# A hybrid decoder step on one core: token halves of 512 and 520 in the seven-product scheme, other PSUM chains, no sums on GpSimd from the gated part on

## The chip, the cores and the metric

The kernel runs on one core of one Trainium2 chip, in one launch. The metric is the device time in microseconds. A program of this kernel keeps five engines in step by semaphores: TensorE (PE; the weight loads are listed apart as PEld), VectorE (DVE), ScalarE (ACT), GpSimd (POOL) and SyncE (SP, which here only issues DMAs).

## What is computed

One decoder layer for a prompt of 1024 tokens and 8 sample tokens (1032 columns in all), with D_MODEL = 1024 and a feed-forward width D_FF = 2816, in float32:

```python
h = rmsnorm(x, g_mix); u = h @ w_in                       # pool branch, conv branch (value, gate)
ya = pool_mixer(...); yb = conv_mixer(...)                # windows of 2/4/8/16; width-31 depthwise conv, LayerNorm, swish
x = x + concatenate([ya, yb]) @ w_out
x = x + cross_attn(rmsnorm(x, g_attn), mk, mv, w_q, w_o)  # 4 heads, 256 memory tokens
h = rmsnorm(x, g_ffn)
x = x + (silu(h @ w_gate) * (h @ w_up)) @ w_down
y = rmsnorm(x, g_final)                                   # also returned: new pool/conv states, memory keys and values
```

## The kernel before

Channels lie on the 128 partitions, tokens on the free axis: first the 512 even prompt tokens, then the 512 odd ones, then the 8 samples. A matrix product takes a weight block of 128x128 as the stationary operand and a stretch of tokens as the moving one. Each float32 operand is split into a high part and a low rest, and each product is three passes (`PASSES`: high x high, high x low, low x high), so each block of a product is three MATMULs per stretch of tokens. `split` (L363 for the high part, L374 for the rest) makes the two parts on ACT, DVE or GpSimd; `split_by_dma` (L385, L392) makes the rest by two ACT passes and a DMA that GpSimd issues and that adds the original in memory.

The program has four stages.

- **Early.** Input projection, pooling, convolution, output projection, attention with its own small path for the samples, and the projection `w_o` (`proj_o`, tile `po`). Most products here take 1032 tokens as three stretches of 344 (tiles `ps`, `oa`, `ob`, `po`, line L471). Keys and values of the memory are products of 256 and 512 columns (tiles `kps`, L841, and `vps`, L918).
- **Gated** (`first_two`, `sixth`, `others` for the first two feed-forward tiles, `seven` for the other twenty). Gate and up projection of one feed-forward tile of 128 channels are a 2x2 block product: two halves of the 1024 input channels, two halves of the 1032 tokens, outputs gate and up. The scheme of Strassen and Winograd makes it of seven products in place of eight, each of 4 weight blocks, three passes and 516 tokens. A product's 516 tokens are two MATMULs of 258 (`TQ`) into two PSUM banks. The products are named A11, A12, A22, S1 to S4, after their token blocks (tiles `ab`, by index: 0 A12, 1 A22, 2 S4, 3 S1, 4 A11, 5 S2, 6 S3). Sums of weights (`wTa`, `wTb`) and of products make up for the missing eighth.
- **Down** (`down`, 16 units: 4 chunks of hidden channels, `c`, by 4 pairs of output tiles, `p`). The first 2048 hidden channels go through the same scheme with w_down: seven products of two weight blocks each, tiles `pr` from `hb` (hidden blocks read back from DRAM) with `dW` (plain weights) and `dV` (summed weights). The results gather in `x2` (printed `x` or `x_0` to `x_3`) and `pp`.
- **Last** (`last_down`, `final`). The other six hidden tiles (`ho`) go through plain products (tile `fd`) in three spans of tokens, `LAST_SPANS`, each followed by its final norm and stores.

The order on every engine is made at build time. The program first lists tasks, each with the engines that could run it and a cost; `Program.order` then walks a model of time, and gives each engine its next task by readiness, room in the buffers and priority. `ORDER` lists the pieces of the early stage; `BIAS`, `LEAD`, `SLACK` and `MARGINS` set how early weights are fetched and prepared and how far costs are trusted. A task that may run on DVE or GpSimd goes where the model ends it first. PSUM has eight banks: two buffers `mm` of three banks and two `ms` of one bank. `product` takes an `mm` buffer, or each third time two `ms` buffers ("narrow", one per 258 tokens); with `onto` it adds a second product onto a PSUM buffer that still holds an earlier one, after the earlier sum has been read out.

Lines that matter below: L1312 is the MATMUL of `product`, L1646 that of `last_down`; L1328 is the DVE instruction that reads a product from PSUM and adds it to a sum, L1332 the ACT copy from PSUM; L1336 (`combine`) and L1354 (`times`) are sums and products of two SBUF operands; L1266 the sums of gate and up weights, L1487 those of the down weights.

## Time and profile before

| | us |
|---|---|
| median of 3 runs (1241.48 to 1244.19) | 1242.89 |
| time of the profiled execution | 1243.26 |
| its span, first to last instruction | 1241.5 |
| PE busy in the span | 1213.6 |
| DVE busy | 887.5 |
| ACT busy | 540.2 |
| GpSimd busy | 461.5 |

The profiled execution's time is 1.8 us above its span. The page gives busy time by engine, the span in 40 slices, the DMA queues, the chain that ended last and groups of instructions; the trace answers further questions by window, by line, by tile and by wait. A busy PE is one with MATMULs in flight, back to back or not: how fast they follow each other must be read from a count of instructions in a stretch.

### The profile page before, as it was taken

The numbers are of one execution on the slowest core, as the hardware profiler recorded it, in microseconds if no ns is written. First come the engines' busy times: TensorE is split into PE (matmuls) and PEld (weight loads), VectorE is DVE, ScalarE is ACT, GpSimd is POOL, SyncE is SP. The second block draws the span as 40 slices with busy tenths as digits, with TensorE's granted clock in tenths as the row PEclk, the third lists the DMA queues.
The fourth block names the chain that finished last, engine by engine and source line by source line (L and its number), as shares of the span: only waits on it lengthen the run. The fifth ranks groups of instructions, "written<-read, shape, count | busy, mean of one in ns | idle before, by whom it ended". The sixth has DMA issues, their size and how long they took to land.

```text
span 1241.5 us, 21913 instructions
## 1 busy us (share of the span) xinstructions
PE 1213.6 (98%) x8946; PEld 1189.8 (96%) x8946; DVE 887.5 (71%) x1449; ACT 540.2 (44%) x749; POOL 461.5 (37%) x386
## 2 busy tenths in 40 slices
PE   8999998999999999999999999999999999998997
PEld 8999987999999889999999999999999999998996
DVE  7999997566368885679786677667655757767444
ACT  7766555553134624453333233323333454442533
POOL 3668741422100012215331223223333269887401
PEclk9999999999999999999999999999999999999999
DMA  7335696455384674331333123321323696867712
GB/s 283 90 66 137 149 243 212 140 133 204 116 250 161 225 295 120 119 103 61 118 114 111 67 105 111 103 103 69 120 70 119 240 288 190 217 190 173 154 56 81
DMA packets 59012, 183.33 MB, mean 148 GB/s; under 512 B 7904, under 2 KB 11680, under 8 KB 57632
## 3 DMA queue, kind: packets, MB, share of 16 engines
q1 hardware_dynamic: 52288, 157.74, 37.1%
q0 software_dynamic: 6624, 24.19, 11.0%
q8 instruction: 70, 1.15, 0.4%
q14 instruction: 30, 0.25, 0.1%
HBM read 148.27 MB, written 33.64 MB: 147 GB/s over the span
## 4 chain that ended last, share of the span: by engine, by line
PE 87%; DVE 4%; DMA 4%; issue 3%; ACT 2%; POOL 1%; SPq 0%; DVEq 0%; ACTq 0%; POOLq 0%
PE pr L1312 47%; PE ps L471 14%; PE po L471 7%; PE fd L1646 5%; PE oa L471 4%; PE ob L471 4%; PE kps L841 1%; PE sc L1017 1%; PE pv L1075 1%; PE vps L918 1%; DMA ho<-hd 1%; DVE spcache_k L1114 1%; DMA raw<-in_w_out_a 1%; DMA sbcache_v<-pd 1%; DMA out_mem_v<-vf 0%
## 5 line engine op out<-in xcount | busy, mean ns | idle before, releaser
L1312 PE MATMUL pr<-ab,wTa 128*128 128x258 f32 x1056 | 134.2, 283 | 0.0
L1312 PE MATMUL pr<-ab,wTb 128*128 128x258 f32 x1056 | 133.7, 283 | 0.0
L1312 PE MATMUL pr<-ab,wG 128*128 128x258 f32 x1056 | 131.2, 283 | 1.0 <-ACT wU L363 0.8
L1312 PEld LDWEIGHTS pr<-ab,wTa 128*128 128x128 f32 x1056 | 130.0, 190 | 0.1
L1312 PEld LDWEIGHTS pr<-ab,wG 128*128 128x128 f32 x1056 | 128.6, 190 | 1.5 <-ACT wU L363 1.1
L1312 PEld LDWEIGHTS pr<-ab,wTb 128*128 128x128 f32 x1056 | 129.8, 190 | 0.0
L471 PE MATMUL ps<-xop,w 128*128 128x344 f32 x720 | 113.9, 320 | 0.0
L471 PEld LDWEIGHTS ps<-xop,w 128*128 128x128 f32 x720 | 113.3, 188 | 0.0
L1312 PE MATMUL pr<-hb,dV 128*128 128x258 f32 x768 | 99.9, 286 | 3.5 <-DVE x L1328 3.5
L1312 PEld LDWEIGHTS pr<-hb,dV 128*128 128x128 f32 x768 | 96.3, 192 | 4.2 <-DVE x L1328 3.9
L1328 DVE TENSOR_TENSOR su<-pr,su 128x516 f32<-128x516 f32 (+1 forms) x98 | 53.2, 560 | 64.3 <-PE pr L1312 62.5
L471 PE MATMUL ps<-xq,w 128*128 128x344 f32 x576 | 94.4, 321 | 0.0
L471 PE MATMUL po<-oo,w 128*128 128x344 f32 x576 | 91.2, 320 | 0.3 <-DVE oo L1080 0.3
L471 PEld LDWEIGHTS po<-oo,w 128*128 128x128 f32 x576 | 90.9, 188 | 0.5 <-DVE oo L1080 0.5
L471 PEld LDWEIGHTS ps<-xq,w 128*128 128x128 f32 x576 | 90.6, 188 | 0.1
L374 POOL TENSOR_TENSOR wU<-gr,wU 128x512 fp32r<-128x512 f32 x19 | 31.9, 1676 | 128.4 <-DVE su L1328 83.5
L1328 DVE TENSOR_TENSOR x<-pr,x 128x258 f32<-128x258 f32 (+1 forms) x102 | 54.2, 553 | 32.4 <-PE pr L1312 31.7
L675 DVE SCALAR_TENSOR_TENSOR cacc<-glu,vec,cacc 128x511 f32<-128x511 f32 (+14 forms) x116 | 77.0, 738 | 0.0
L1312 PE MATMUL pr<-hb,dW 128*128 128x258 f32 x576 | 74.7, 283 | 0.0
L1332 ACT ACTIVATE su<-pr 128x516 f32<-128x516 f32 (+1 forms) x63 | 37.4, 595 | 79.1 <-PE pr L1312 79.1
L1312 PEld LDWEIGHTS pr<-hb,dW 128*128 128x128 f32 x576 | 71.7, 189 | 0.0
L1646 PE MATMUL fd<-ho,w 128*128 128x258 f32 x576 | 70.1, 283 | 1.6 <-DMA ho<-hd 1.6
(328 smaller groups left out, 2403.3 us busy)
## 6 DMA issues: line engine op xcount, KB each, us to landing
gr<-in_w_gu SPq DMA_DIRECT2D x44, 512.0 KB, 3.4
hs<-hb SPq DMA_DIRECT2D x28, 516.0 KB, 4.6
hb<-su SPq DMA_DIRECT2D x8, 1032.0 KB, 6.6
dr<-in_w_dn SPq DMA_DIRECT2D x16, 512.0 KB, 6.0
hb<-hb POOLq DMA_DIRECT2D x12, 516.0 KB, 9.2
spcache_k<-in_cache_k SPq DMA_DIRECT2D x12, 512.0 KB, 4.8
raw<-in_w_in SPq DMA_DIRECT2D x10, 512.0 KB, 3.4
x<-in_xT SPq DMA_DIRECT2D x8, 516.0 KB, 6.3
```

The source lines that it names most:

```text
L374: e.tensor_tensor(dst(1), src(), f32(dst(0)), ALU.subtract)
L471: e.matmul(ps[:, c, :CW], w[:, wi, cols], x[:, xi, c * CW : (c + 1) * CW], start=first and p == 0, stop=last and p == 2)
L675: e.scalar_tensor_tensor(acc[h][:, n:], src[:, : HALF - n], w, acc[h][:, n:], ALU.mult, ALU.add)
L841: e.matmul(ps[:, 0, i * NMEM : (i + 1) * NMEM], w[:, wi, block_cols(k)], memg[k // 4][:, xi, k % 4], start=(k == 0 and p == 0), stop=(k == ...
L918: e.matmul(ps[:, m], memg[k // 4][:, xi, k % 4, m * P : (m + 1) * P], w[:, wi, col : col + 512], start=(k == 0 and p == 0), stop=(k == KT ...
L1017: e.matmul(bank()[:, i * NMEM : (i + 1) * NMEM], qop[2 * h + dt][:, qi, tt * P : (tt + 1) * P], kk[:, ki, 2 * (h % 2) + dt], start=(dt == ...
L1075: e.matmul(ps[:, c], v[:, vi, m, col : col + P], pT[h][m][:, pi, sl], start=(m == 0 and p == 0), stop=(m == 1 and p == 2))
L1114: e.scalar_tensor_tensor(piece[:, b], piece[:, b], 1.0, bc[:, b], ALU.mult, ALU.mult, accum_out=out(m)[:, first + b : first + b + 1])
L1312: e.matmul(bank(c), w[:, wi, cols(j)], xs[0](j, xi)[:, c * TQ : (c + 1) * TQ], start=onto is None and j == 0 and p == 0, stop=j == nj - 1 ...
L1328: from_sums(sums, "DVE", dve, lambda e, src, sl: e.tensor_tensor(as_banks(o(sl), src), src, as_banks(a(sl), src), ALU.add), [akey], [okey])
L1332: from_sums(sums, "ACT", lambda n: act(n, True), lambda e, src, sl: e.activation(as_banks(o(sl), src), src, AF.Copy), [], [okey])
L1646: e.matmul(view(i), w[:, wi, col : col + P], hops[k][:, xi, lo + i * width // count : lo + (i + 1) * width // count], start=(k == 0 and p ...
```

## The change

Four things change together.

1. **Halves.** The two token halves are 512 (the even tokens) and 520 (odd tokens and samples) in place of twice 516. Blocks A11, A12 and S4 are 512 wide, one MATMUL into one bank; S1, S2, S3 and A22 are 520 wide, two MATMULs of 260. The 8 sample columns have no partner in the first half, so small instructions patch them (`samples`, `zeros`). The spans of the last stage are 512, 260 and 260 in place of 516, 258 and 258.
2. **PSUM chains.** In `seven` the sequence of products becomes A11, S1, S2, A12 onto A11, S3 onto S2, S4, A22 onto S2. In `down` A12 goes onto A11, and every other product has its own buffer. The 512-wide products use the one-bank buffers; the 520-wide ones two banks of an `mm` buffer. No product is "narrow" any more. DVE reads S2 from PSUM where ACT copied it.
3. **GpSimd.** After the early stage a flag (`state["alone"]`) leaves the splits to ACT (high part) and DVE (rest), and the sums in `combine` and of the gate and up weights to DVE. GpSimd keeps the DMAs that add in memory, some sums of the down weights, some squares and small memsets.
4. **Order.** `ORDER` has other numbers and now includes the pieces of the `w_o` projection and of the start of the gated stage; `BIAS`, `LEAD`, `SLACK`, `MARGINS` and the list of weights split by DMA (`BY_DMA`) are new. Some model costs change, which moves instructions but computes nothing. `ones_c` goes; `ones_d` with a factor of 2 stands in for it.

The core of the diff:

```diff
-BY_DMA = {"w_in": (3, 4, 5, 7, 9, 10), "w_k": (1, 2, 5, 7), ..., "w_v": (0, 1, 3, 4, 7), "w_dn": (17, 18, 19), "w_dn2": (1,)}
-LAST_SPANS = ((0, 516), (516, 258), (774, 258))
+BY_DMA = {"w_in": (3, 4, 6, 7, 9, 10, 11), "w_k": (2, 3, 5, 6), ..., "w_v": (0, 7), "w_dn": (17, 18, 19), "w_dn2": (1,)}
+LAST_SPANS = ((0, 512), (512, 260), (772, 260))
...
-TH = T // 2
-TQ = TH // 2
+HW = (HALF, T - HALF)
+TW = HW[1]
+WIDTH = [HALF if b in (A11, A12, S4) else TW for b in range(7)]
-DOWN_ORDER = (A11, A12, S1, S2, S3, S4, A22)
+DOWN_ORDER = (A11, S1, A12, S2, S3, S4, A22)
...
+    def either(n):
+        return {"DVE": dve(n)} if state.get("alone") else {"Pool": pool_tt(n), "DVE": dve(n)}
...
-        if not ps:
+        if not ps and not state.get("alone"):
             hi["Pool"] = pool_ts(n)
...
-        if gain is None and not ps:
+        if gain is None and not ps and not state.get("alone"):
             lo["Pool"] = pool_tt(n)
...
-    def product(w, cols, xs, steps=1, onto=None, narrow=None):
+    def product(w, cols, xs, width, steps=1, onto=None, single=ms_buf):
...
+        nj, count = len(xs[1]), 1 + (width > 512)
+        n = width // count
...
-                    for c in range(2):
-                        e.matmul(bank(c), w[:, wi, cols(j)], xs[0](j, xi)[:, c * TQ : (c + 1) * TQ],
+                    for c in range(count):
+                        e.matmul(bank(c), w[:, wi, cols(j)], xs[0](j, xi)[:, c * n : (c + 1) * n],
...
     def seven(f):
-        one = of_tokens(G, 0, A11, narrow=False)
-        copy_sums(part(f, 0), (k, 0), one)
-        plus(f, 0, 0, of_tokens(G, 512, A12, narrow=True))
-        gated(f, 0)
-        of_tokens(Ta, 0, S2, onto=one)
-        copy_sums(part(f, 2), (k, 2), one)
-        two = of_tokens(Tb, 0, S1, narrow=False)
-        copy_sums(part(f, 3), (k, 3), two)
-        of_tokens(Ta, 512, S3, onto=one)
+        start(f, 1)
+        plus(f, 1, 3, of_tokens(Tb, 0, S1))
+        one = of_tokens(Ta, 0, S2)
+        plus(f, 3, 2, one)
+        first = of_tokens(G, 512, A12, onto=firsts[f])
+        plus_sums(part(f, 0), (su[f], 0), factors(0), RF[0], first, ALU.mult)
+        activated(f, 0)
+        of_tokens(Ta, 512, S3, onto=one)
         plus(f, 3, 3, one)
-        of_tokens(U, 0, S4, onto=two)
-        plus(f, 2, 2, two)
+        plus(f, 2, 2, of_tokens(U, 0, S4))
         start_kept(f)
         times_value(f, 0)
         of_tokens(Tb, 512, A22, onto=one)
...
     def down(u):
         first = plain(A11, lambda j: 2 * j * P)
-        into(0, first)
-        into(0, plain(A12, lambda j: (2 * j + 1) * P))
-        fifth = summed(S1, 0)
-        into(4, fifth)
-        summed(S2, 2, first)
-        into(3, first, True)
+        into(3, first, True)
+        into(4, summed(S1, 0))
+        plain(A12, lambda j: (2 * j + 1) * P, first)
+        into(0, first)
+        into(3, summed(S2, 2))
         into(5, summed(S3, 3), True)
-        plain(S4, lambda j: 512 + j * P, fifth)
-        into(2, fifth)
+        into(2, plain(S4, lambda j: 512 + j * P))
         if c == CHUNKS - 1:
             both(p, 2, 2, 3)
+            both(p, 2, 2, 4)
         into(1, summed(A22, 1))
...
+    pg.margin, state["alone"] = MARGINS["gated"], True
```

What this does to the order on the engines shows at three places. The first is PE in one feed-forward tile of the gated stage (`pr` is PSUM, `ab_` the token blocks, of which each product takes two tiles; `wTa`, `wTb`, `wU`, `wG` the weights). Before, from S2 on, in the order S2, S1, S3, S4, A22 and then A11 of the next tile:

```order
L1312 MATMUL pr_7402<-ab_0_4714,wTa_7221 128x258 x12
L1312 MATMUL pr_7402<-ab_1_5118,wTa_7221 128x258 x12
L1312 MATMUL pr_7493<-ab_0_4699,wTb_7314 128x258 x12
L1312 MATMUL pr_7493<-ab_1_5144,wTb_7314 128x258 x12
L1312 MATMUL pr_7402<-ab_0_4702,wTa_7221 128x258 x12
L1312 MATMUL pr_7402<-ab_1_5132,wTa_7221 128x258 x12
L1312 MATMUL pr_7493<-ab_0_4730,wU_7395 128x258 x12
L1312 MATMUL pr_7493<-ab_1_5156,wU_7395 128x258 x12
L1312 MATMUL pr_7402<-ab_0_4655,wTb_7314 128x258 x12
L1312 MATMUL pr_7402<-ab_1_5035,wTb_7314 128x258 x12
L1312 MATMUL pr_7620<-ab_0_4603,wG_7485 128x258 x12
L1312 MATMUL pr_7620<-ab_1_4934,wG_7485 128x258 x12
```

Now, from S1 to A22:

```order
L1323 MATMUL pr_6530<-ab_0_4695,wTb_6459 128x260 x12
L1323 MATMUL pr_6530<-ab_1_5173,wTb_6459 128x260 x12
L1323 MATMUL pr_6563<-ab_0_4711,wTa_6452 128x260 x12
L1323 MATMUL pr_6563<-ab_1_5198,wTa_6452 128x260 x12
L1323 MATMUL pr_6512<-ab_0_4641,wG_6449 128x512 x6
L1323 MATMUL pr_6512<-ab_1_5145,wG_6449 128x512 x6
L1323 MATMUL pr_6563<-ab_0_4708,wTa_6452 128x260 x12
L1323 MATMUL pr_6563<-ab_1_5186,wTa_6452 128x260 x12
L1323 MATMUL pr_6639<-ab_0_4729,wU_6503 128x512 x6
L1323 MATMUL pr_6639<-ab_1_5204,wU_6503 128x512 x6
L1323 MATMUL pr_6563<-ab_0_4625,wTb_6459 128x260 x12
L1323 MATMUL pr_6563<-ab_1_5130,wTb_6459 128x260 x12
```

Three of the seven products are half as many MATMULs, twice as wide; one buffer (`pr_6563`) takes S2, S3 and A22 in turn, with one 512-wide product between each two of them.

The second place is GpSimd, late in the down stage (`x_0`, `x_1` and `pp` are output sums, `ho` the last hidden tiles, `dt`, `dV`, `dW` down weights). Before:

```order
L374 TENSOR_TENSOR dW_11760<-dr_11599,dW_11760 128x256
L392 DMA ho_11779<-hd 128x1032
L1336 TENSOR_TENSOR x_0_9857<-x_0_9857,pp_9888 128x516
L1336 TENSOR_TENSOR pp_9888<-x_1_9955,pp_9888 128x516
L1336 TENSOR_TENSOR x_1_9955<-x_1_9955,pp_9888 128x516
L1336 TENSOR_TENSOR x_1_9955<-pp_9888 128x516
L374 TENSOR_TENSOR w_11880<-raw_11709,w_11880 128x1024
```

Now:

```order
L1506 TENSOR_TENSOR dt_10558<-dr_10385,dt_10558 128x256
L402 DMA ho_10599<-hd 128x1040
L402 DMA ho_10698<-hd 128x1040
L402 DMA ho_10766<-hd 128x1040
L402 DMA ho_10791<-hd 128x1040
L1506 TENSOR_TENSOR dt_10819<-dr_10526,dt_10819 128x256
L402 DMA w_10869<-in_w_dn 128x1024
```

The sums of outputs and the splits have gone to DVE, and the six DMAs for `ho` follow each other with short sums between them.

The third place is PE where the down stage gives way to the last. Before, the end of the last unit's A22 and the start of the first `fd` product:

```order
L1312 MATMUL pr_0_11991<-hb_1_11453,dV_11742 128x258
L1312 MATMUL pr_1_11992<-hb_1_11453,dV_11742 128x258
L1646 MATMUL fd_0_12011<-ho_11525,w_11880 128x258 x6
L1646 MATMUL fd_0_12011<-ho_11550,w_11880 128x258 x6
L1646 MATMUL fd_0_12011<-ho_11655,w_11880 128x258 x6
L1646 MATMUL fd_0_12011<-ho_11779,w_11880 128x258 x6
L1646 MATMUL fd_0_12011<-ho_11898,w_12005 128x258 x6
L1646 MATMUL fd_0_12011<-ho_11918,w_12005 128x258 x6
```

Now, the last unit's S4 and A12, then an `fd` product, then the unit's S1, S2, S3 and A22:

```order
L1323 MATMUL pr_10797<-hb_2_10419,dW_10685 128x512 x6
L1323 MATMUL pr_10784<-hb_0_10183,dW_10685 128x512 x6
L1660 MATMUL fd_1_10821<-ho_10491,w_10805 128x512 x3
L1660 MATMUL fd_1_10821<-ho_10512,w_10805 128x512 x3
L1660 MATMUL fd_1_10821<-ho_10698,w_10805 128x512 x3
L1660 MATMUL fd_1_10821<-ho_10599,w_10805 128x512 x3
L1660 MATMUL fd_1_10821<-ho_10766,w_10817 128x512 x3
L1660 MATMUL fd_1_10821<-ho_10791,w_10817 128x512 x3
L1323 MATMUL pr_10856<-hb_3_10096,dV_10841 128x260 x12
L1323 MATMUL pr_10872<-hb_5_10285,dV_10841 128x260 x12
L1323 MATMUL pr_10892<-hb_6_10401,dV_10841 128x260 x12
L1323 MATMUL pr_10909<-hb_1_10430,dV_10841 128x260 x12
```

The first `fd` product now stands ahead of four products of the last unit that need the summed weights `dV`.

More of the change, by code (lines that the diff above doesn't have):

```diff
@@ L1189, in proj_o @@
         ps = mm_buf(f"po{n}")
-        for spans in ((0, 1), (2,)) if n in O_ORDER[:2] else ((0, 1, 2),):
+        for spans in ((0, 1), (2,)) if n in (0, 4) else ((0, 1, 2),):
             for k in range(KT):
@@ L1443, in seven @@
         of_tokens(Tb, 512, A22, onto=one)
-        o = part(f, 1)
-        from_sums(one, "DVE", dve, lambda e, src, sl: e.tensor_tensor(
-            as_banks(o(sl), src), src, as_banks(Rf[:, TH + sl.start : TH + sl.stop], src), ALU.mult), RF, [(k, 1)])
-        add({"ACT": act(TH)}, lambda e: e.activation(o(), o(), AF.Silu), [(k, 1)], [(k, 1)], func=AF.Silu)
-        times(f, 1, lambda: Rf[:, TH:], RF)
+        plus(f, 1, 1, one)
+        gated(f, 1)
         times_value(f, 1)
```

308 lines of the change are left out of this document (152 added, 156 removed), and 9 rows, old and new, of the table ORDER.

## The prediction

> **What bounds the kernel now.** I read the page's busy times first, then the clock by slices, the windows of the four stages, the waits of PE, and last the chain that ended last, for the pace of MATMULs.
>
> ```profile
> PE 1213.6 (98%) x8946; PEld 1189.8 (96%) x8946; DVE 887.5 (71%) x1449; ACT 540.2 (44%) x749; POOL 461.5 (37%) x386
> PEclk9999999999999999999999999999999999999999
> 0.00:545.00 545.00, 531.56 (x3327) 511.56 (x3328) 411.11 (x801) 276.88 (x388) 179.87 (x191) 1.00 0.57 171
> 545.00:1010.00 465.00, 464.79 (x3852) 463.23 (x3852) 332.56 (x421) 168.79 (x232) 152.47 (x85) 1.00 0.33 114
> 1010.00:1165.00 155.00, 149.91 (x1223) 148.99 (x1222) 111.49 (x171) 63.85 (x76) 119.19 (x99) 0.99 0.75 200
> 1165.00:1242.00 77.00, 67.34 (x550) 65.99 (x548) 32.35 (x59) 30.71 (x56) 9.96 (x13) 0.96 0.28 77
> ```
>
> The columns of a window are its length, then PE, PEld, DVE, ACT and GpSimd busy with their instructions, the granted clock, the DMA share and GB/s. The clock is full all along, and PE is busy 98% of the span. From 545 to 1010 us it misses 0.2 us. So time can go in two ways only: MATMULs that follow each other faster, or the few places where PE waits. These are (waiting engine and tile, who ended the wait, us in total, times, longest):
>
> ```profile
> PE psg L471 <- ACT w L363: 5.0, 1, 5.0
> PE kps L841 <- ACT vf L923: 1.9, 1, 1.9
> PE pmap L861 <- ACT yf L865: 1.9, 1, 1.9
> PE pt L1056 <- DVE pT L1061: 1.1, 2, 0.6
> PE sc L1017 <- ACT probs L1034: 0.9, 1, 0.9
> PE vps L918 <- DMA w<-in_w_v: 0.9, 1, 0.9
> PE pr L1312 <- ACT wU L363: 0.8, 1, 0.8
> PE pr L1312 <- DVE x L1328: 3.5, 2, 3.2
> PE fd L1646 <- DMA ho<-hd: 1.6, 1, 1.6
> ```
>
> The first is the start of the program and stays. The next six, 7.5 us, lie in the early stage, the last two, 5.1 us, in the down stage and at its end.
>
> **Part 1, the halves of 512 and 520.** The pace comes from stretches of the chain in which PE waits for nobody (start, us, what, count): 256 columns (`kps`), 512 (`vps` and `pv`), 344 (`ps`) and 258 (`pr`).
>
> ```profile
> 147.69 11.46 PE kps L841 x96
> 159.15 11.13 PE vps L918 x48
> 412.88 2.79 PE pv L1075 x12
> 49.83 97.86 PE ps L471 x621
> 554.47 471.09 PE pr L1312 x3914
> ```
>
> One MATMUL takes 11.46 / 96 = 119.4 ns with 256 columns, 11.13 / 48 = 231.9 ns with 512. The line through both is 0.4395 ns for a column and 6.9 ns for the MATMUL itself. It gives 120.3 ns at 258 columns, where 471.09 / 3914 is 120.4, and 158.1 at 344, where 97.86 / 621 is 157.6; so it holds. Width costs what it did; only the 6.9 ns is saved, once for each MATMUL that goes. How many there are, by line 1312 and line 1646 alone (PE busy, count, clock):
>
> ```profile
> 0.00:1242.00 1242.00, 609.72 (x5040) 1.00 0.49 148
> 0.00:1242.00 1242.00, 70.11 (x576) 1.00 0.49 148
> ```
>
> That is 5616 MATMULs of 258 columns. In the changed program A11, A12 and S4 are 36 of a tile's MATMULs, the other four products 96, where all seven were 168; over 22 tiles 3696 become 2904. In a down unit 84 become 18 + 48; over 16 units 1344 become 1056. The last stage's 576 become 144 + 288. In all 1224 fewer: 1224 x 6.9 = 8.4 us saved. The columns rise by 48 a tile and 24 a unit, 1440 in all, which costs 0.6 us. Net **-7.8 us**, all on the path, since PE waits for nobody there. The bounds: the fixed part is 8.6 ns by the slope between the 258 and 344 rows, 5.5 ns by that between 344 and 512, so -9.9 to -6.1 us (`pv`, 2.79 / 12 = 232.5 ns, lies between). I take the line, because it alone meets all four widths within 0.5 ns.
>
> The Trainium skill, page "TensorE: Matmul & The Clock Gate", section "Wait — 56ns, not 53.3ns?", puts a warm MATMUL at its columns over 2.4 GHz plus about 2.5 ns, 215.7 ns at 512 columns; by that the saving would be 1224 x 2.5 ns less the columns, some 2.5 us by estimate. The trace has 231.9 ns and does not agree; it returns below as a rival.
>
> **Part 2, GpSimd without sums.** The 3.2 us wait, in order of time (start, us, engine, line, what):
>
> ```profile
> 1134.30 6.20 DVE L1336 TENSOR_TENSOR x<-x 128x516 f32<-128x516 f32 x1
> 1136.93 1.79 POOL L1336 TENSOR_TENSOR x<-x,pp 128x516 f32<-128x516 f32 x1
> 1138.18 1.76 POOL L1336 TENSOR_TENSOR pp<-x,pp 128x516 f32<-128x516 f32 x1
> 1141.16 4.54 PE L1312 MATMUL pr<-hb,dV 128*128 128x258 f32 x24 [3.18 <-DVE x L1328]
> ```
>
> A DVE sum of two SBUF operands runs 6.2 us while GpSimd runs sums and splits back to back; the PSUM reads queue behind it on DVE, and PE has no free bank. Such a sum alone takes 0.69 us (below). In the changed program these GpSimd instructions are gone from this place, and the DVE sum should fall to 0.7 us. **-3.2 us**. The bounds are -3.5 (the whole row of waits) and 0 (if something else is late next: DVE now has the sums of `x` and `pp` itself, four of 0.69 us for each pair of output tiles).
>
> The Trainium skill, page "SBUF — State Buffer", section "Who interferes with whom", says that a DVE instruction with two SBUF inputs contends with a GpSimd instruction that reads SBUF. The trace agrees: of the rows below the weight sum at 512 columns takes 1921 ns in the mean, the PSUM read of 516 columns takes 691.
>
> What DVE takes over must fit beside PE. Rows of 580 to 980 us (busy, mean ns, idle before), and the window inside the gated stage:
>
> ```profile
> L1445 DVE TENSOR_TENSOR su<-pr,Rf 128x516 f32<-128x516 f32 x19 | 13.1, 691 | 14.0 <-PE pr L1312 14.0
> L374 DVE TENSOR_TENSOR wTa<-ta,wTa 128x1024 fp32r<-128x1024 f32 x17 | 20.8, 1221 | 9.0 <-ACT wTa L363 9.0
> L374 DVE TENSOR_TENSOR wU<-gr,wU 128x512 fp32r<-128x512 f32 x3 | 2.1, 684 | 0.0
> L1266 DVE TENSOR_TENSOR ta<-tb,gr 128x512 f32<-128x512 f32 x16 | 30.7, 1921 | 0.0
> 560.00:780.00 220.00, 220.00 (x1831) 219.89 (x1830) 166.95 (x204) 72.42 (x98) 72.88 (x38) 1.00 0.29 99
> DVE su L1328 <- PE pr L1312: 60.2, 47, 2.6
> ```
>
> A gated tile now asks of DVE: 6 PSUM reads, 5 products, on average 2 sums for the hidden blocks and 4 weight sums, 17 x 0.69 = 11.7 us; the rests of three weights of 1024 and one of 512, 3 x 1.22 + 0.68 = 4.3 us; together 16.1. PE needs 36 x 0.2319 + 96 x 0.1212 = 20.0 us. That is 81%, where the window has 166.95 / 220 = 76% with fewer instructions that GpSimd stretches. ACT has three splits of 1024, one of 512, a copy and two activations, under 7 us. The added work hides behind PE, and DVE waited for PE, 60 us of 400, not PE for DVE: **0**. If that cover were gone, each us of DVE over 20.0 a tile would cost 22 us.
>
> In the down stage the margin is thinner:
>
> ```profile
> 1010.00:1142.00 132.00, 128.48 (x1057) 127.78 (x1056) 96.62 (x148) 52.62 (x65) 108.61 (x92) 1.00 0.77 208
> L1328 DVE TENSOR_TENSOR x<-pr,x 128x258 f32<-128x258 f32 x41 | 15.6, 419 | 4.1 <-PE pr L1312 3.7
> L1487 POOL TENSOR_TENSOR dt<-dr 128x256 f32<-128x256 f32 x10 | 9.8, 979 | 6.5 <-DMA dr<-in_w_dn 5.8 <-POOL dV L374 0.4
> ```
>
> A unit asks of DVE 7 reads x 0.69, rests of 1024, 512 and 256 columns (1.22 + 0.68 + 0.42), three quarters of a hidden block's rest (0.9) and 1.4 weight sums of 256 columns (0.6): 8.7 us, against 18 x 0.2319 + 48 x 0.1212 = 10.0 of PE, 87%.
>
> **Part 3, the PSUM chains.** In a gated tile DVE reads S2 out while A12 runs (12 x 0.2319 = 2.8 us) before S3 may go onto it; the same for S3, during S4. Before, the cover was one product of 24 x 0.1204 = 2.9 us, and PE never waited: **0**; if DVE had two rests of 1.22 us ahead of the read, 2 x 1.22 + 0.69 = 3.1 us, PE would wait 0.3. In a down unit A12 goes onto A11 after S1 alone, 12 x 0.1212 = 1.5 us, where 2.9 us lay before. A read of 0.69 fits, one behind a rest of 1.22 does not, by 0.5 us; the order already puts another product between in some units. Between 0 and 16 x 0.5 = 8 us I take **+1.0**, near the lower end, because in the old down stage PE lost only 3.5 us while GpSimd stretched DVE's work.
>
> **Part 4, the order.** Up to the gated stage the instructions are the same in kind and nearly in number, and PE's products stand in nearly the same sequence. Some of the 7.5 us of waits will move and others come; from -7.5 to +7.5 I take **0**, since an order made by the same kind of model leaves waits of the same kind. At the end of the down stage an `fd` product goes ahead of four products of the last unit. It needs all six `ho` tiles, and the last of these landed thus:
>
> ```profile
> 1153.37 10.78 DMA ho<-hd
> ```
>
> PE waited 1.6 us for it. Now ACT and GpSimd reach these tiles earlier in their queues (no weight split and no sums ahead), while PE asks for them four products, 5.8 us, earlier: between -1.6 and +5.8, I take **0**. The tail after the last MATMUL is unchanged but for widths of 260 in place of 258.
>
> **Sum.** -7.8 - 3.2 + 1.0 = -10.0 us from the profiled execution's 1243.26 (1.8 above its span) is 1233.3; that execution lies 0.4 above the median, so against 1242.89 the forecast is **1233 us**.
>
> **Rivals.** (a) *DVE becomes the bound of the down stage.* 41 weight sums stay on GpSimd there. If each blocks a DVE sum or rest for its whole 0.98 us, that is 2.5 us a unit; DVE then needs 11.2 us, PE 10.0, and 16 x 1.2 = 19 us are lost in place of the 1.0: 1251. It decides once DVE loses over 1.3 us a unit. Against it: about half of DVE's time there is PSUM reads, which show no stretching (419 ns for 258 columns here, 691 for 516 in the gated stage), and GpSimd was busy 108.6 of 132 us and cost 3.5. (b) *The new early order loses* as much as the old waits hold: 1241, no change. (c) *It wins* them: 1225. For either only the list of waits speaks. (d) *The last unit waits for `ho`*, its S1, S2, S3 and A22 queued behind: 1239. For it speaks the 10.8 us landing, against it the emptier GpSimd queue. (e) *The wider MATMULs save less:* if one of 512 columns took 4.5 ns more in these products than the 231.9 ns of `vps`, part 1 would lose 1224 x 4.5 = 5.5 us and the time be 1238. For it speaks only that no product of the gated stage has that width yet; against it that `pv`, another kind of product, has 232.5. The Trainium skill's rule named in part 1 ends at this time too.
>
> **Chances.** Forecast 0.59 (its own range, by the bounds of part 1 and of the chains, 1229 to 1237), (a) 0.06, (b) 0.12, (c) 0.10, (d) 0.08, (e) 0.05. The range of 1225 to 1240 leaves out (a), and half of (b) and of (c), 0.17. A measurement of this kernel can tell 0.2%, 2.5 us, from no change. Below 1240.4 lie the forecast, (c), (e), most of (d) and under half of (b): 0.86 faster; the rest of (b) and (d) is the same, 0.08; (a) is slower, 0.06.
>
> **What the new profile would show.** Part 1: the 5040 MATMULs of `product` become 2880 of 260 columns at 121 ns and 1080 of 512 at 232 ns, and a gated tile takes 20.0 us. Part 2: no DVE sum of 520 columns over 1 us in the last units, and no 3 us wait of PE there; GpSimd nearly idle in the gated stage, DVE near 80%. Part 3: waits of PE for DVE in the down stage of about 1 us in all. Part 4: early waits near 7 us. Wrong would be a 512-wide MATMUL at 240 ns, or PE idle in the gated stage.

## The result, and the profile after

The changed kernel takes 1226.30 us (median of 4 runs, 1225.38 to 1228.28); the kernel before, run beside it on the same chip, 1242.18 (1241.17 to 1244.19). The ratio is 0.9872, with a 95% interval of 0.9854 to 0.9891. The forecast was 1233 in 1225 to 1240: the direction and the range were right, but the gain was 15.9 us and not 10, and the time lies below the forecast's own range of 1229 to 1237.

The profiled execution after took 1225.38 us, 17.9 less than the profiled one before. Its busy times:

```profile
PE 1199.8 (98%) x7720; PEld 1122.3 (92%) x7720; DVE 927.9 (76%) x1546; ACT 528.3 (43%) x722; POOL 246.3 (20%) x299
PEclk9999999999999999999999999999999999999998
```

There are 8946 - 7720 = 1226 matrix instructions fewer: the 1224 of the prediction, and two of four columns for the final norm (`fin_ps`), which a span of 516 needed and one of 512 does not. GpSimd is busy 246 us in place of 462. PE is at 98% as before: the program is as full of MATMULs as it was, and has fewer. Where PE still waits (engine and tile, who ended it, us in total, times, longest):

```profile
PE psg L480 <- ACT w L373: 5.1, 1, 5.1
PE pr L1323 <- DVE x L1339: 2.1, 1, 2.1
PE pv L1081 <- DVE oo L1086: 1.8, 2, 1.2
PE Rf_ps L510 <- DVE xss L411: 1.8, 1, 1.8
PE psg L480 <- DVE xop L386: 1.2, 1, 1.2
PE pmap L870 <- ACT yf L874: 0.9, 1, 0.9
```

The 3.2 us and the 1.6 us of the late stages are gone; a new 2.1 us stands in the down stage, and a new 1.8 us (`Rf_ps`) just after the first product of the gated stage. Two windows follow, the gated one of before and the down one (length, then PE, PEld, DVE, ACT, GpSimd, the clock, DMA):

```profile
560.00:780.00 220.00, 220.00 (x1477) 203.11 (x1477) 171.30 (x241) 62.22 (x81) 1.85 (x17) 1.00 0.28 99
1010.00:1142.00 132.00, 129.72 (x828) 117.49 (x828) 110.51 (x161) 64.45 (x75) 39.48 (x46) 0.99 0.73 192
```

DVE is at 171.30 / 220 = 78% in the gated stage and 110.51 / 132 = 84% in the down stage (the prediction had 81 and 87), and PE waits for nobody in the first. The stretch of the gated stage in the chain that ended last, and then the order of products on PE, each row with its start:

```profile
547.44 438.44 PE pr L1323 x2928
```

```profile
604.10 2.94 PE L1323 MATMUL pr<-ab,wG 128*128 128x512 f32 x12
606.88 3.03 PE L1323 MATMUL pr<-ab,wTb 128*128 128x260 f32 x24
609.75 3.03 PE L1323 MATMUL pr<-ab,wTa 128*128 128x260 f32 x24
```

438.44 / 2928 = 149.74 ns, times the 132 MATMULs of a tile is 19.77 us, where before 168 x 471.09 / 3914 = 20.22. From start to start, 12 MATMULs of 512 columns take 2.78 us, 231.7 ns each, as the line of the prediction had it (230.8 in the mean over the stage). 24 of 260 take 2.87 us, 119.6 ns each, where it had 121.2.

The stages' ends come from the first starts in the list of the tile `pr` (count, ns, first and last start), here of the changed kernel:

```profile
L1323 PE MATMUL pr<-ab,wG x528: 387/392/476, 540.4 to 971.3; 128*128 128x512 f32 x176
L1323 PE MATMUL pr<-hb,dW x288: 387/393/628, 980.1 to 1137.0; 128*128 128x512 f32 x144
```

The same rows of the other kernels give this table (us; each of one profiled execution):

| kernel | before the gated stage | gated | down and last | span |
|---|---|---|---|---|
| before | 543.4 | 447.2 | 250.8 | 1241.5 |
| after | 540.4 | 439.7 | 243.5 | 1223.6 |
| e2, sums on GpSimd in both stages | 541.2 | 454.6 | 246.7 | 1242.5 |
| e8, in the down stage alone | 545.2 | 439.7 | 246.9 | 1231.8 |
| e11, in the gated stage alone | 544.9 | 453.2 | 243.2 | 1241.3 |
| e3, before with no sums on GpSimd | 542.3 | 452.0 | 250.1 | 1244.4 |
| e4, old early order | 547.7 | 440.4 | 242.1 | 1230.2 |

So the change brought 3.0 us in the early stage, 7.5 in the gated one and 7.3 behind it.

### The profile page after: what moved, and what is told of

Same layout as the page of the kernel before. It is cut to its first block, busy times and chain, and to the rows that moved or that the text cites. A ratio compares the mean times of both kernels' runs of the same rounds, so it can differ in the third digit from the quotient of the medians.

```text
span 1223.6 us, 19409 instructions
## 1 busy us (share of the span) xinstructions
PE 1199.8 (98%) x7720; PEld 1122.3 (92%) x7720; DVE 927.9 (76%) x1546; ACT 528.3 (43%) x722; POOL 246.3 (20%) x299
## 4 chain that ended last, share of the span: by engine, by line
PE 74%; DVE 5%; DMA 4%; issue 1%; ACT 1%; POOL 0%; SPq 0%; DVEq 0%; ACTq 0%; POOLq 0%
PE pr L1323 46%; PE po L480 7%; PE fd L1660 5%; PE ps L480 5%; PE oa L480 4%; PE ob L480 4%; PE sc L1023 1%; DMA x<-x2d 1%; DMA w<-in_w_q 1%; PE pv L1081 1%; DVE spcache_k L1120 1%; DMA spcache_k<-in_cache_k 1%; PE kps L850 0%; DVE w L384 0%; DMA sbcache_k<-qd 0%
## 5 line engine op out<-in xcount | busy, mean ns | idle before, releaser
L1323 PE MATMUL pr<-ab,wTa 128*128 128x260 f32 x1056 | 133.6, 282 | 0.0
L1323 PE MATMUL pr<-ab,wTb 128*128 128x260 f32 x1056 | 133.3, 282 | 0.0
L1323 PE MATMUL pr<-ab,wG 128*128 128x512 f32 x528 | 128.8, 393 | 0.0
L1339 DVE TENSOR_TENSOR su<-pr,su 128x520 f32<-128x520 f32 (+1 forms) x112 | 77.6, 695 | 57.3 <-PE pr L1323 57.1
L1323 PE MATMUL pr<-hb,dV 128*128 128x260 f32 x768 | 100.7, 284 | 2.1 <-DVE x L1339 2.1
L1323 PE MATMUL pr<-hb,dW 128*128 128x512 f32 x288 | 75.4, 399 | 0.0
L1660 PE MATMUL fd<-ho,w 128*128 128x260 f32 (+1 forms) x432 | 69.6, 321 | 0.2
L1660 PEld LDWEIGHTS fd<-ho,w 128*128 128x128 f32 x432 | 61.7, 188 | 7.8 <-DVE w L384 1.1
L373 ACT ACTIVATE w<-raw 128x1024 fp32r<-128x1024 f32 (+1 forms) x35 | 32.9, 944 | 76.3 <-issue 20.0
L1323 PE MATMUL pr<-ab,wU 128*128 128x512 f32 x264 | 64.8, 394 | 0.0
```

Source lines behind the costliest of these rows:

```text
L373: e.activation(dst(0), src(), AF.Copy, scale=1.0 if gain is None else gain)
L1323: e.matmul(bank(c), w[:, wi, cols(j)], xs[0](j, xi)[:, c * n : (c + 1) * n], start=onto is None and j == 0 and p == 0, stop=j == nj - 1 an ...
L1339: from_sums(sums, "DVE", dve, lambda e, src, sl: e.tensor_tensor(as_banks(o(sl), src), src, as_banks(a(sl), src), op), [akey], [okey])
L1660: e.matmul(view(i), w[:, wi, col : col + P], hops[k][:, xi, half, lo - half * HALF + i * width // count : lo - half * HALF + (i + 1) * wid ...
```

## The experiments

Each kernel was timed against the kernel before on its own chip; its ratio is to be held against 0.9872. The medians of the kernel before on these chips lie between 1242.2 and 1243.0 us, so that differences of medians between chips can be off by about 1 us, besides the spread of the runs.

### e1: 512 columns as two MATMULs of 256

```diff
-                    for c in range(count):
-                        e.matmul(bank(c), ..., xs[0](j, xi)[:, c * n : (c + 1) * n], ...)
+                    for c in range(2):
+                        half = n // 2
+                        out = bank(c) if count == 2 else bank(0)[:, c * half : (c + 1) * half]
...
```

> The changed kernel, with each MATMUL of 512 columns in the products of the gated, down and last stages issued as two of 256 columns into the same bank: 1224 MATMULs more, nothing else moved. Theory 1 (a MATMUL costs 6.9 ns besides its columns, and PE is the bound): 1224 x 6.9 = 8.4 us more than the changed kernel, 1234 to 1235 us, with 119 to 120 ns for a MATMUL of 256. Theory 2 (only some 2.5 ns a MATMUL, and the rest of the gain is from elsewhere): 3 us more, 1229. Theory 3 (the count of MATMULs does not matter): 1226.

It took 1233.54 us, ratio 0.992 (0.9906 to 0.9935): +7.2 us over the changed kernel by medians, 6.0 by the ratios, with 1224 MATMULs more. The chain's gated stretch:

```profile
546.31 444.84 PE pr L1326 x3720
```

444.84 / 3720 = 119.58 ns. By start times a MATMUL of 256 takes 119.5 ns, so the pair takes 239.0 where one of 512 takes 230.8: 8.2 ns for each MATMUL more, and the gated stage, with 792 more, is 6.3 us longer (539.3 to 985.2 us). The total is less than 1224 x 8.2 = 10.0 us because a wait in the down stage is shorter here (1.3 us in place of 2.1, and no clock stretch behind it, see e10). Theory 1 is the nearest: the count of MATMULs has its price. But the kernel before, with almost the same count, took 1242: the count alone is not the change.

### e12 and e13: 256 and 258 of the 260 columns

```diff
-                        e.matmul(bank(c), w[:, wi, cols(j)], xs[0](j, xi)[:, c * n : (c + 1) * n],
+                        m = 256 if count == 2 and (j or p or onto is not None) else n
+                        e.matmul(bank(c)[:, :m], w[:, wi, cols(j)], xs[0](j, xi)[:, c * n : c * n + m],
```

(e13 has 258, in the gated stage alone.)

> The changed kernel with the 260-column MATMULs of the gated and the down stage cut to their first 256 columns (all but the first that opens each chain), which leaves the last four columns of each stretch out of the sums; the places where they begin stay. Theory 1 (the line of the prediction holds, 0.44 ns a column): 4 x 0.44 = 1.76 ns less for each of some 2700 MATMULs, 4.7 us faster, about 1221.5 us. Theory 2 (256 and 260 columns take the same 119.5 ns, as the run with 512 in two of 256 let them): 1226 us, no change.

> The changed kernel with the 260-column MATMULs of the gated stage cut to their first 258 columns (all but the first that opens each chain), which leaves the last two columns of each stretch out of the sums; the stretches begin where they did. With 260 columns they take 119.6 ns, with 256 from the same starts 117.8; the 258 of the kernel before took 120.2 in the mean and 119.8 with the second stretch moved to column 260. Theory 1 (the pace from these starts goes by columns alone, and the rest of the difference lies in the layout): 118.7 ns, 2024 x 0.9 = 1.8 us faster, about 1224.5 us. Theory 2 (a length of 258 itself, no multiple of four columns, costs about 1.1 ns): 119.8 ns, about 1226.5 us.

e12 took 1221.63 us, ratio 0.982 (0.9796 to 0.9844), e13 1225.31, ratio 0.987 (0.9821 to 0.9919). The chain's gated stretch of e12, then of e13:

```profile
547.71 435.15 PE pr L1324 x2928
```

```profile
548.80 438.67 PE pr L1324 x2928
```

The mean over all widths is 149.74 ns with 260 columns (after), 149.82 with 258, 148.62 with 256. The first two are equal; from 260 to 256 the mean falls by 1.12, and since 92 of a tile's 132 MATMULs were cut that is 1.12 x 132 / 92 = 1.6 ns for each. By start times the cut ones take 117.8 ns with 256 columns and 119.7 with 258, beside 119.6 for 260. Theory 1 of e12 and theory 2 of e13 hold: a MATMUL of 258 columns takes as long as one of 260. So two more columns in each MATMUL would have cost the halves of 516 nothing.

The changed kernel now has a line of its own: 119.6 ns at 260 columns and 230.8 at 512 are 0.441 ns for a column and 4.9 ns for the MATMUL. It gives 117.8 ns at 256, where e12 measured 117.8, and 118.7 at 258. The 258-column MATMULs of the kernel before took 120.2 in the mean, 1.5 ns more.

### e5: the kernel before, its second stretch moved to column 260

```diff
-    ab = [[op_r(f"ab{b}_{jj}", (P, 2, 2, TH)) for jj in range(2)] for b in range(7)]
+    ab = [[op_r(f"ab{b}_{jj}", (P, 2, 2, 2, 260)) for jj in range(2)] for b in range(7)]
```

(This kernel also drops `ones_c` and a small tile, as the changed kernel does; the down stage keeps its old layout.)

> The kernel before, with the second 258-column stretch of each gated block moved from column 258 (1032 bytes) to column 260 (1040 bytes) of its tile; widths and counts as before. Theory 1 (a stretch that begins at a multiple of 8 but not of 16 bytes costs the pair of MATMULs 3 ns): the gated MATMULs go from 120.3 to 118.7 ns without alternating, 3696 x 1.6 = 5.8 us, 1236.5 us; the down stage keeps 120.6 ns. Theory 2 (pace goes by columns alone, and the 260-column MATMULs of the changed kernel are quicker for another reason): 1242 us, and the pairs still alternate by 3 ns.

It took 1241.44 us, ratio 0.9986 (0.9971 to 1.0001): inconclusive in time. The chain shows a part of what theory 1 wanted:

```profile
554.81 478.17 PE pr L1313 x3986
```

478.17 / 3986 = 119.96 ns, where it was 471.09 / 3914 = 120.36. By start times the two MATMULs of a pair took 118.5 and 121.9 ns before, and 119.3 and 120.3 in e5. The uneven pair goes with the start of the second stretch; the mean falls by 0.4 ns only, 3696 x 0.4 = 1.5 us, and the gated stage is 1.6 us shorter (543.8 to 989.4). Theory 1's 5.8 us were wrong. Of the 1.5 ns by which a MATMUL of 258 lags behind the line above, its start thus makes 0.4 and the width itself 0.9 (e13: 119.7 against 118.7); 0.2 are left over.

### e2, e8 and e11: the sums back on GpSimd

```diff
-    pg.margin, state["alone"] = MARGINS["gated"], True
+    pg.margin, state["alone"] = MARGINS["gated"], False
```

(e2 as here. e8 sets the flag to False where the down stage begins to be prepared, e11 in the gated stage alone.)

> The changed kernel with GpSimd allowed splits and sums again after the early stage. Theory 1 (taking GpSimd out removed stretched DVE sums that PE waits for in one or two places only): PE stays without idle time in the gated stage, DVE sums of several us come back, and the loss is 0 to 4 us, 1226 to 1230. Theory 2 (the GpSimd part carried much of the gain): 6 us or more lost, over 1232. Theory 3 (DVE alone is the tighter bound): faster than 1225.

> The changed kernel with GpSimd allowed sums and splits again from the preparation of the down stage on, not in the gated stage. Theory 1 (its sums hurt mostly in the gated stage, where they stretch DVE's own sums and make the PSUM reads late): the gated stage takes 439.7 us as in the changed kernel, the down stage about 3 us longer: 1229.5 us. Theory 2 (they hurt in the down stage, where the wait of the kernel before stood): 1236 us or more, with PE waits of over 2 us there.

> The changed kernel with GpSimd allowed sums and splits in the gated stage, and not from the preparation of the down stage on: the complement of the run in which they were allowed in the down stage alone. Theory 1 (the losses are local to the stages and add up): the gated stage 454.6 us as in the run with GpSimd in both, the down stage as in the changed kernel: 1226.3 + 14.9 = about 1241 us. Theory 2 (it is the two together that overload DVE): under 1234 us.

e2 took 1243.27 us, ratio 1.0006 (0.9987 to 1.0024): the whole gain is gone. e8 took 1232.26, ratio 0.9899 (0.9865 to 0.9932), e11 1238.23, ratio 0.996 (0.9944 to 0.9976). The table above shows the losses in place: 14.9 us of e2 and 13.5 of e11 lie in the gated stage, 3.2 of e2 and 3.4 of e8 behind it, and they add up. So theory 2 of e2 holds, and of e8 and e11 theory 1 is the nearer. (The profiled execution of e8 lost 4.8 us more in the early stage, where PE waited 2.7 us for a weight load with a half-clock stretch of 3.4 us behind it; its runs lie between 1229.0 and 1233.6. The profiled execution of e11, 1243.08 us, is the slowest of its ten.) How one of the gated waits comes about in e2, in order of time:

```profile
681.86 3.09 DVE L384 TENSOR_TENSOR wG<-gr,wG 128x1024 fp32r<-128x1024 f32 x1 [0.45 <-ACT wG L373]
683.82 3.37 POOL L384 TENSOR_TENSOR wTb<-tb,wTb 128x1024 fp32r<-128x1024 f32 x1
684.87 2.87 DVE L1347 TENSOR_TENSOR su<-su,Rf 128x512 f32<-128x512 f32 x1
687.66 1.28 DVE L1339 TENSOR_TENSOR su<-pr,su 128x520 f32<-128x520 f32 x2
688.40 3.89 PE L1323 MATMUL pr<-ab,wTb 128*128 128x260 f32 x18 [2.06 <-DVE su L1339]
```

While GpSimd makes one weight rest, DVE's product of two SBUF operands takes 2.87 us; alone, in the changed kernel, such a product takes 0.69. The PSUM read stands behind it on DVE, and PE wants to put its next product onto that bank. Over the gated stage, the same groups in the window 580 to 960 us of e2 and of the changed kernel (busy, mean ns):

```profile
L384 DVE TENSOR_TENSOR wG<-gr,wG 128x1024 fp32r<-128x1024 f32 x12 | 22.2, 1853 | 5.4 <-ACT wG L373 5.4
L384 DVE TENSOR_TENSOR wTa<-ta,wTa 128x1024 fp32r<-128x1024 f32 x12 | 20.8, 1731 | 0.0
```

```profile
L384 DVE TENSOR_TENSOR wTa<-ta,wTa 128x1024 fp32r<-128x1024 f32 x19 | 23.2, 1221 | 0.0
L384 DVE TENSOR_TENSOR wG<-gr,wG 128x1024 fp32r<-128x1024 f32 x19 | 23.2, 1221 | 3.1 <-ACT wG L373 3.1
```

12 rests take DVE about as long as 19 do when GpSimd is out: what GpSimd takes over, DVE loses again while it runs beside it. The PSUM reads themselves are not stretched: those of 512 and 520 columns take 0.69 us in the mean in e2, 0.70 at most. The waits of PE in the gated stage of e2:

```profile
PE pr L1323 <- DVE su L1339: 9.1, 5, 2.3
```

9.1 us of waits explain only part of 14.9. The rest is in the clock, below (e10).

Behind the gated stage the loss is of another kind. In the down stage of e8 PE waits for a PSUM read 0.9 us at most. It waits for the last `ho` instead, and so it does in e2 (3.1 us). The wait, and GpSimd's queue ahead of the DMA:

```profile
PE fd L1660 <- DMA ho<-hd: 3.3, 1, 3.3
1140.58 0.73 POOL L1506 TENSOR_TENSOR dt<-dr 128x256 f32<-128x256 f32 x1 [0.93 <-DVE w L384]
1142.08 0.86 POOL L402 DMA_DIRECT2D ho<-hd  x1
```

ACT had done its part of all six `ho` by 1136.89 us, but GpSimd, behind sums and a wait for DVE, issues the last DMA 5.2 us later; in the changed kernel it does so 0.3 us behind ACT.

### e3: the kernel before, GpSimd without sums

```diff
+    def either(n):
+        return {"DVE": dve(n)} if state.get("alone") else {"Pool": pool_tt(n), "DVE": dve(n)}
...
-    pg.margin = MARGINS["gated"]
+    pg.margin, state["alone"] = MARGINS["gated"], True
```

> The kernel before, with GpSimd kept out of sums and splits from the gated part on, as in the changed kernel; halves, chains and order as before. Theory 1 (the old chains gave every read a cover of 2.9 us, so GpSimd's sums cost only the one 3.2 us wait and the half-clock stretch of 3.4 us behind it, 1.7 us): 1242.3 - 4.9 = 1237.4 us, the gated stage as long as before. Theory 2 (GpSimd's sums cost 17 us in any scheme, as the run of the changed kernel with them has it): about 1226 us. Theory 3 (without GpSimd, DVE is too slow for the old scheme of more and smaller reads): slower than 1242 us.

It took 1244.81 us, ratio 1.0012 (0.9994 to 1.0031), no change within the noise. This piece of the change, alone, gains nothing: theories 1 and 2 fall, and what theory 3 said of a late DVE shows at two places only. Its waits in the gated and the down stage:

```profile
PE pr L1315 <- DVE x L1331: 4.4, 3, 2.1
PE pr L1315 <- DVE wTa L377: 3.2, 1, 3.2
```

The first gated tiles need their weights at once, and DVE, now alone with the rests, is 3.2 us late at 574.86 us; from there to the end of the stage PE waits for nobody. In the down stage the 3.2 us wait has only moved (2.1 us, and two shorter ones). (The clock on record for this execution is 0.949 all along, outside its two half-clock stretches, where the other traces have 1.0; its gated MATMULs take the same 120.2 ns.) So taking GpSimd out is worth nothing in the old scheme and 17 us in the new one (e2 against the changed kernel). What makes the new scheme so dependent was not tried: the widths, the chains, or the order, whose numbers (`MARGINS`, `BIAS`, `SLACK`) e2 keeps as they were set for the kernel without GpSimd, and e3 as they were set for the one with it.

### e4: the early order of before

```diff
-    "m5 A3 n0 g1 v1 g2 v2 m3 m7 m4 C0 g3 v3 C1 m0 ...
+    "m3 n0 m0 m2 A3 g1 v1 C0 g2 v2 C1 g3 m5 m1 ...
```

(`ORDER` up to the projection `w_o`, `BY_DMA` and `LEAD` as before.)

> The changed kernel with the early order of before (the old list of pieces up to the w_o projection, the old lists of weights split by DMA and their leads). Theory 1 (the new early order is worth what the traces differ by up to the first gated product, 543.4 against 540.4 us): the first gated product starts 3 us later, 1229. Theory 2 (an accident of that execution, or gained by the other edits): 1226 to 1227.

It took 1232.07 us, ratio 0.9906 (0.9889 to 0.9924), 5.8 us more than the changed kernel by medians and 4.2 by the ratios, more than theory 1 had. The early waits of e4:

```profile
PE pmap L869 <- ACT yf L873: 1.8, 1, 1.8
PE kps L849 <- ACT vf L931: 1.5, 1, 1.5
PE kps L849 <- DVE w L383: 1.4, 1, 1.4
PE pv L1080 <- ACT probs L1039: 1.3, 2, 0.9
PE ob L479 <- DVE opb L383: 1.1, 2, 0.5
```

The new order is worth 4 to 6 us in the kernel that it was made for. Against the kernel before it is less: there the gated stage began at 543.4 us, in e4 at 547.7. In the three profiles with the old program up to there (before, e3, e5) it began at 542.3 to 543.8 us, in the ten with the new one at 539.3 to 545.2, which is 1.4 us earlier in the mean; so one pair of profiles tells this term to some 3 us only.

### e6 and e9: the new wait in the down stage

The 2.1 us wait, in order of time: DVE's subtraction, and the transfer in the chain of waits.

```profile
1011.99 0.69 DVE L1347 TENSOR_TENSOR x<-x,pp 128x512 f32<-128x512 f32 x1 [3.31 <-DMA x<-x2d]
1012.60 0.68 DVE L1339 TENSOR_TENSOR x<-pr,x 128x512 f32<-128x512 f32 x1
```

```profile
997.48 14.43 DMA x<-x2d
1014.88 121.17 PE pr L1323 x786
```

The subtraction patches the samples for the halves of 512 and 520. It stands ahead of the unit's PSUM reads on DVE and waits for a load issued 14.4 us earlier. e6 moves it to the end of the unit, where it subtracts a later state of its operand, so that the sums of the odd half are others; e9 computes all, and issues the loads a unit earlier.

```diff
-            both(p, 2, 2, 4, ALU.subtract)
...
+        if not c:
+            both(p, 2, 2, 4, ALU.subtract)
```

```diff
+            later(lambda: x2_load(0), "load")
...
+            if u < 3:
+                later(lambda: x2_load(u + 1), "load")
```

> The changed kernel with the new subtraction of the odd sample part, which DVE does ahead of a unit's first read in chunk 0, put behind the unit's last read. Theory 1 (PE's 2.1 us wait at 1012 us came from DVE standing at this subtraction until the load of x landed): the wait goes, 1224. Theory 2 (the reads that follow need loads of the same group, so the wait only changes its name): 1226.

> The changed kernel with the loads of x2d for the first four down units issued a unit earlier, so that the subtraction of unit 0 finds its operand there; it computes all that the reference does. Theory 1 (the 2.1 us wait and the half-clock stretch behind it, 1.7 us, go): 1226.3 - 3.8 = 1222.5 us. Theory 2 (the wait was hardly in the median: moving the subtraction gave 1226.8): 1226 us.

e6 took 1226.80 us, ratio 0.9875 (0.9849 to 0.9902), with runs from 1223.5 to 1229.8: inconclusive in time, though its profiled execution (1223.53 us) has neither the wait nor a half-clock stretch in the down stage. e9 took **1222.69 us** (5 runs, 1221.35 to 1223.82), ratio 0.983 (0.9807 to 0.9854), and beats both kernels. The row of `x` is gone from its waits. The gain is 3.6 us by medians and 5.2 by the ratios, and between the two profiled executions 3.0 us from the first gated product on: about what theory 1 said, 2.1 of wait and 1.7 of clock.

### e10: waits of known places

```diff
+STALLS = {5: 4, 7: 7, 9: 10, 11: 13, 13: 16, 15: 20, 17: 25}
...
+        for _ in range(STALLS.get(f, 0)):
+            add({"DVE": 0.01}, lambda e: e.tensor_scalar(part(f, 3)(), part(f, 3)(), 1.0, 1.0, ALU.mult, ALU.mult), ...)
         plus(f, 3, 2, one)
```

> The changed kernel with 4, 7, 10, 13, 16, 20 and 25 extra DVE instructions (520 columns times one, in place) ahead of the reads of S2 in the tiles 5, 7, 9, 11, 13, 15 and 17 of the gated stage, so that PE waits there for different lengths of time; nothing computed changes. Theory 1 (a PE wait of about 2 us or more is followed by one clock stretch of 3.4 us at half speed, a shorter one is not): such a stretch behind each of the longer waits and none behind those under 1.5 us, and the gated stage longer by the waits plus 1.7 us for each stretch. Theory 2 (the stretches come by themselves, and long waits fell beside them by chance): no more than one in the gated stage, and the stage longer by the waits alone.

It took 1243.79 us, ratio 0.9997 (0.9979 to 1.0015). The extra instructions take 0.43 us each. Seven of them (3.0 us) made PE wait nowhere, ten (4.3 us) for 1.1 us. Two of the waits, one shorter and one longer than 2 us, and the granted clock (after the five busy times) in the 3.4 us behind these and three more:

```profile
737.74 3.13 PE L1324 MATMUL pr<-ab,wTa 128*128 128x260 f32 x24 [1.11 <-DVE su L1340]
780.07 4.67 PE L1324 MATMUL pr<-ab,wTa 128*128 128x260 f32 x24 [2.48 <-DVE su L1340]
```

```profile
737.80:741.20 3.40, 3.40 (x27) 3.32 (x28) 3.40 (x5) 0.64 (x1) 0.11 (x1) 1.00 0.01 2
780.30:783.70 3.40, 3.40 (x17) 3.40 (x17) 3.19 (x4) 0.63 (x1) 0.00 (x0) 0.50 0.00 0
825.40:828.80 3.40, 3.40 (x26) 3.14 (x26) 3.40 (x5) 1.16 (x2) 0.11 (x1) 1.00 0.00 0
869.10:872.50 3.40, 3.40 (x16) 3.30 (x15) 3.33 (x8) 0.00 (x0) 0.00 (x0) 0.51 0.53 158
913.40:916.80 3.40, 2.95 (x7) 2.37 (x8) 3.40 (x7) 0.13 (x1) 0.00 (x0) 0.50 0.44 152
```

After waits of 1.1 us (at 737.74 and 825.37) the clock stays full; after 2.48, 2.12 and 2.57 it is halved for 3.4 us, and 24 MATMULs of 260 columns take 4.67 us in place of 3.03. The gated stage is 999.7 - 542.8 = 456.9 us, 17.2 more than in the changed kernel: 12.3 of waits, by start times, and 3 x 1.7. Theory 1 holds for these waits. So it is in e2, where such stretches stand behind three of the five gated waits: 10.0 us of waits by start times + 3 x 1.7 = 15.1, and the stage is 14.9 us longer. The kernel before has one behind its 3.2 us wait, the changed kernel one behind its 2.1, e9 none.

The length of a wait alone does not decide it, though. In each of the 14 traces the changes of the clock lie on a grid of 3.413 us, with another offset in each trace. In e11 three gated waits are equally long (2.07, 2.08 and 2.07 us), and only the second has a stretch behind it. Here are the cells of the grid in which each began, and the next ones (PE busy is the first number behind the length):

```profile
688.44:691.85 3.41, 1.62 (x7) 0.96 (x6) 3.41 (x3) 0.63 (x1) 3.41 (x3) 1.00 0.45 151
691.85:695.27 3.42, 3.14 (x25) 3.15 (x26) 1.51 (x3) 0.00 (x0) 0.74 (x1) 1.00 0.48 141
770.36:773.77 3.41, 1.32 (x6) 0.75 (x6) 3.41 (x3) 0.63 (x1) 3.41 (x3) 1.00 0.45 154
773.77:777.18 3.41, 3.41 (x17) 3.41 (x18) 1.06 (x2) 0.00 (x0) 0.29 (x1) 0.50 0.50 151
852.28:855.69 3.41, 2.28 (x10) 1.51 (x8) 3.41 (x2) 0.63 (x1) 3.41 (x3) 1.00 0.41 141
855.69:859.10 3.41, 2.47 (x20) 2.47 (x21) 2.17 (x4) 0.00 (x0) 1.41 (x1) 1.00 0.32 90
```

PE is idle for 1.79, 2.09 and 1.13 us of the first cell: only the second wait lies in one cell from end to end. From the first change of the clock to the last MATMUL the 14 traces have 4972 such cells. All 18 that are followed by half clock have PE idle for 1.87 us or more; of the others one has 1.90 us, and no other over 1.80. The third stretch of e10 thus belongs to two waits, 2.57 and 1.60 us, which share the cell ahead of it.

## Why the prediction was right, and where its sizes were not

The sum was -10.0 us. The terms, measured between the two profiled executions, start to start on PE (a clock stretch is counted with the wait ahead of it):

| step | predicted | measured |
|---|---|---|
| Part 1, halves | -7.8 | -13.2 |
| Part 2, the wait behind the stretched sum | -3.2 | -5.0 |
| Part 3, later PSUM reads in the down stage | +1.0 | +3.4 |
| Part 4, early order with the first gated tile | 0 | -1.8 |
| Part 4, `fd` ahead of the last unit | 0 | -1.3 |
| sum | -10.0 | -17.9 |

**Part 1 had the right mechanism, but it was only a part of what happened**, and its size lies beyond its own bound of -9.9. The gated stage gave 8.9 us (predicted 5.0; a tile of 168 x 120.2 ns became 36 x 230.8 + 96 x 119.6), the down stage 3.1 (1.8), the last stage 1.2 (1.0). The 512-wide MATMULs came at 231 to 232 ns, as said, and rival (e) is out. The step that failed is the line "120.3 ns at 258 columns ... so it holds", carried on to 121.2 at 260. The line met 120.3 by chance: 258 columns cost what 260 do (e13), and the second stretch's start cost 0.4 ns besides (e5). By the line of the changed kernel's own rows (e12), about 3.4 us of the gated stage's gain are the fewer MATMULs, and about 5.5 (3696 x 1.5 ns) the lag of the 258-column ones, which the prediction did not have. That the lag and the line's fixed part of 6.9 ns, too large against 4.9, erred in opposite ways kept the sum as near as it was. The slope itself holds between 256 and 260 (117.8 to 119.6). The Trainium skill's columns over 2.4 GHz plus about 2.5 ns (page "TensorE: Matmul & The Clock Gate", section "Wait — 56ns, not 53.3ns?") would give, by estimate, 215.8 ns at 512 and 110.8 at 260, against 230.8 and 119.6 here: the runs do not agree with it.

**Part 2** named the right wait. The wait is gone, and the sums of 520 columns take 0.70 us in the mean in the changed down stage, as said. That it went because GpSimd's sums went is not shown: without them the old kernel still waits there (e3, 2.1 us with a clock stretch), and with them in the new down stage PE waits for a read 0.9 us at most (e8). Two things were missing. The half-clock stretch behind the wait, 1.7 us, went with it. And the term was priced by the waits that the old scheme had; e2 shows that in the new scheme the same GpSimd sums would cost 17 us, and e3 that without the new scheme the term is worth nothing. It is no term that can be added to the others. The rule of the Trainium skill, page "SBUF — State Buffer", section "Who interferes with whom", that a DVE instruction with two SBUF inputs contends with a GpSimd one that reads SBUF agrees with 2.87 against 0.69 us in e2. The claim that DVE's added work hides behind PE in the gated stage came true: 78% busy, no wait.

**Part 3**: the gated chains cost 0, as said. The down chains cost nothing that the trace shows either; the one wait there, 2.2 us by start times and 1.7 of clock, less 0.5 that went, belongs to the subtraction that waits for its load. The prediction read the order of the products and not the new small instructions on DVE, nor what they wait for; e9 took this wait away. Rival (a) did not come: the down stage has fewer GpSimd instructions (39 us of 132 busy, not 109), and with more of them back (e8) the 3.4 us lost are no overloaded DVE but the wait for `ho`.

**Part 4**: that 0 was wrong is not shown, since the end of the new early stage varies by 6 us between executions. The early waits fell from 7.5 to about 5 us and the stage by 3.0 us, of which the new waits at the first gated products (2.6 us by start times, 1.4 before) took 1.2 back. e4 gives the new order 4 to 6 us against the old one in the new kernel, so rival (c) came true at most in part. The last unit did not wait for `ho` (rival d): the 1.6 us wait is gone. The prediction's reason against (d), the emptier GpSimd queue, is borne out by e2 and e8, where the queue is full again and PE waits 3.1 and 3.3 us for `ho`.

The errors add up to 7.9 us, all but one on the side of more gain. The range held the time near its lower end, which it had for rival (c); what filled it was mostly part 1, so that the range held is in part luck.

## What to carry to other kernels

Price a change of engine by the schedule that it will stand in, not by the waits of the old one: here the same move was worth 0 in the old scheme and 17 us in the new. Count a PE wait of about 2 us or more at up to 1.7 us above its length, and look at the loads of small new instructions on a queue of PSUM reads first. When two widths of MATMUL are compared, measure the pace of just these widths and starts; a line through others missed 1.6 ns in 120, which over the 2112 gated MATMULs of 260 columns is 3.4 us of a gain of 16.

## What the runs showed of the hardware that was not expected

- A MATMUL of 258 columns takes as long as one of 260 (119.7 and 119.6 ns), and one of 256 takes 117.8 in the same place. In the 256-wide pairs of e1, both into one PSUM bank, it took 119.5; why these take 1.7 ns more than e12's is open, and with it 3.4 of the 8.2 ns that each split MATMUL cost in e1.
- With the second stretch at column 258 the MATMULs of a pair alternate, 118.5 and 121.9 ns; at column 260 they nearly do not.
- A busy PE that waits for about 2 us can lose half its clock for 3.4 us. In e2, e3, e10, e11 and the two kernels, gated and down stage, 13 of 16 waits of 2.2 to 3.4 us, measured from start to start, had such a stretch behind them, and of those up to 1.96 us only the one that shared a cell with a longer one. What separates them is how long PE is idle within one cell of a 3.413 us grid: 1.87 us or more in all 18 cells with half clock behind them, 1.90 at most in the 4954 others; the border of a cell cuts each of the three exceptions. The Trainium skill, page "TensorE: Matmul & The Clock Gate", section "HAM oscillation — how this bites in real kernels", warns of PE idle gaps of over about 3.4 us. The stretch has that length here (3.41 us), but gaps of 2.2 us were enough to bring it: the measurement decides.
